# Mixing block of a hybrid decoder step: sample states on VectorE, their outputs as one wide product with ScalarE sums, convolution inputs in one tile

## The chip, the cores and the metric

The kernel runs on one core of one Trainium2 chip. The metric is device time in microseconds (us) of one execution. Five engines work side by side, each through its own queue in order: PE (TensorE, matrix products), DVE (VectorE), ACT (ScalarE), POOL (GpSimd) and SP (the queue that issues most transfers). An engine that waits holds up everything behind it in its queue.

## The reference, cut to what matters

One layer for 256 prompt tokens and 8 sample tokens (264 columns, all processed together): a SwiGLU half step, a mixing block, a second SwiGLU half step, a final norm. The mixing block runs four mLSTM heads and a short gated convolution beside each other. For a sample token, each head b updates a 256 x 256 state C and reads it with the query (one step of `mlstm_chunkwise`, length 1):

```
C_new = decay * C + wk (outer) v
num   = q . C_new
h     = num / max(|den|, exp(-m))
h     = h * rsqrt(mean(h * h) + EPS)          # per head, later gated
u     = gc * xc                               # convolution input
yc    = sum(cw[j] * u_ext[:, j:j + S] for j in range(3)) + conv_b
yb    = gb * yc, then a norm over groups of 128 channels
new_buf = u_ext[:, -2:]
```

The eight samples' states make 4 heads x 8 samples x 256 x 256 float32 values, read and written once.

## The kernel before

All weights come as float32 and are split on chip into two float16 parts: a chunk (usually 128 x 8 blocks x 128) lands in `wraw`, ACT writes the high part `whi` (L178, through `high`), DVE the rest `wlo` (L186, through `low`), and PE multiplies three times per block (`three`, L224 to L226). A product of 16 blocks is two chunks of 24 matmuls. `fetch` issues transfer, `whi` and `wlo` of a chunk up to `AHEAD` (5) chunks before PE uses it; six buffers of each exist.

Everything else is placed among these products by an agenda. `at(delta, fn)` registers work, `product` calls `tick()` at its start and `tick(0.5)` in its middle, and the work due then is written into the engines' queues at that point. So 1 stands for one product, and each engine's order follows from these numbers; when a piece really runs follows from its waits.

In `mix`, the order of products is: the gates; then h0 c0 c1 h1 c2 c3 h2 c4 c5 h3 c6 c7 (a head has six products, two each for q, k and v; a convolution block three) and o0 to o7, then the output projection. Work of a head is spread over the twelve products behind its own:

- `sample_vectors` (L787 on) makes a row `r` of q, wk, decay and 1/den per sample and sends it to memory (`dr`); `sample_rows` loads it back broadcast to all partitions (`rb`); `sample_state` loads two samples' states (`cs`). There are four groups n = 0 to 3 of two samples.
- `sample_update` (L825 on) at 3.5 + 1.5 n: per sample ACT makes two products of wk with v (into `vk` and over wk itself in `rb`) and scales the state by the decay (`cs`, L835), and POOL adds the products (L839, four per group).
- `sample_output` (L841 on) at 5 + 1.5 n: POOL issues the store of `cs`; DVE multiplies the state with q and sums along the row (`jk`, L850, four per group), then multiplies by 1/den into `ha`.
- `squares`, `norm`, `scale` at 10, 11.5 and 12 give the head's norm; the squares are on POOL.

A convolution block makes its input `u` (DVE, with POOL copies of the old rows in and the new rows out), three taps (ACT, then DVE), the product with the gate (`gated`, at 3), the square on ACT (at 3.5), a column sum on PE (`sums`, at 4.5, L353), and the rest of the norm on ACT and DVE (5, 5.5, 6).

POOL's queue also issues the transfers of `dr`, `rb`, `cs` and the states' stores, in the order in which they are written.

Of the kernel before, what the change touches and what calls it, by code (L numbers as in the profile page):

```python
# [16 lines left out]
SEQ = 256  # L17
# [97 lines left out]
def step(ctx: ExitStack, tc: tile.TileContext, a: dict, bad=None):  # L115
# [6 lines left out]
    AHEAD = 5 if half_size else 3  # L122
# [377 lines left out]
def mix(tc, a, nm, n2, h, e):  # L500
# [39 lines left out]
    rows = mp.tile([8, 2 * HD + 2], F32, tag="r", name="rows")  # L540
# [9 lines left out]
    cvp = mp.tile([128, 8, 2], F32, name="cvp")  # L550
    cvs = mp.tile([128, 8, NS, 2], F32, name="cvs")
# [56 lines left out]
    class Head:  # L608
        def __init__(self, hd):
# [26 lines left out]
            self.rb, self.c = [], []  # L636
            for n in range(4):
                at(1.5 + n if n < 3 else 6, self.sample_state, n)
                at(2.5 + n if n < 3 else 6, self.sample_rows, n)
# [37 lines left out]
        def mask_decays(self):  # L677
            for sb, x in enumerate(self.ex):
                nc.gpsimd.affine_select(
                    x, x, pattern=[[1, SEQ - 128 * sb]], compare_op=ALU.is_ge,  # L680
                    fill=0.0, base=0, channel_multiplier=-1,
                )
# [102 lines left out]
        def sample_vectors(self):  # L785
            hd, pq = self.hd, self.pq
            self.vs = vs = mp.tile([128, 2, NS], F32, tag="vs", name="vs", bufs=2)  # L787
            for i in range(2):
                nc.gpsimd.tensor_copy(vs[:, i, :], self.v[i][:, SEQ:T])
            r = mp.tile([8, 2 * HD + 2], F32, tag="r", name="r")  # L790
# [9 lines left out]
            junk = mp.tile([128, HD], F32, tag="jk", name="jk")[:8]  # L800
# [7 lines left out]
            nc.vector.reciprocal(r[:, 2 * HD + 1 : 2 * HD + 2], rdh)  # L808
            nc.vector.tensor_copy(r[:, 2 * HD : 2 * HD + 1], si[:, hd : hd + 1])
            self.dr = tc.dram_tile([8, 2 * HD + 2], F32, name=f"dr{hd}")  # L810
# [10 lines left out]
        def sample_rows(self, n):  # L821
            rb = mp.tile([128, 2, 2 * HD + 2], F32, tag="rb", name="rb", bufs=3)
            nc.gpsimd.dma_start(rb, self.dr[2 * n : 2 * n + 2].partition_broadcast(128))
            self.rb.append(rb)

        def sample_update(self, n):
            rb, c = self.rb[n], self.c[n]
            for b in range(2):
                wk = rb[:, b, HD : 2 * HD]
                vk = mp.tile([128, HD], F32, tag="vk", name="vk", bufs=2)  # L830
                for eb, out in enumerate((vk, wk)):
                    nc.scalar.activation(  # L832
                        out, wk, AF.Copy, scale=self.vs[:, eb, 2 * n + b : 2 * n + b + 1]
                    )
                nc.scalar.activation(  # L835
                    c[:, b], c[:, b], AF.Copy, scale=rb[:, b, 2 * HD : 2 * HD + 1]
                )
                for eb, add in enumerate((vk, wk)):
                    nc.gpsimd.tensor_tensor(c[:, b, eb], c[:, b, eb], add, op=ALU.add)  # L839

        def sample_output(self, n):  # L841
# [4 lines left out]
            num = mp.tile([128, 2, 2], F32, tag="num", name="num", bufs=2)  # L846
            jk = mp.tile([128, HD], F32, tag="jk", name="jk", bufs=1)
# [6 lines left out]
            for eb in range(2):  # L854
                nc.vector.tensor_tensor(
# [222 lines left out]
```

## Time and profile before

| | |
|---|---|
| time, median of 3 runs | 1887.6 us (1887.57 to 1887.67) |
| the profiled execution's own time | 1886.64 us |
| its span, first to last instruction | 1884.9 us |
| PE busy | 1836.8 us, 97% of the span |
| PE's granted clock, mean | 0.990 |
| DVE, ACT, POOL busy | 1193.9, 860.8, 228.7 us |
| mixing block, about | 716 to 1080 us of the span |

A time in a row is counted in us from the span's start. A row of the timeline has start, duration, engine, line of the kernel, operation, the tiles (output <- inputs) with shapes, and in brackets how long the engine had stood idle before it and what ended that. Matmuls overlap: a row shows 0.28 us for a matmul whose successor starts 0.11 us after it. The granted clock is a share of full speed: 1.00 is 2.4 GHz, 0.50 is 1.2 GHz.

### The profile page before, as it was taken

To read this page: it belongs to the slowest core of one execution; us is meant where nothing else is said; L and a number is where in the kernel's file an instruction comes from. 1 tells how busy PE (TensorE), PEld (TensorE's weight loads), DVE (VectorE), ACT (ScalarE), POOL (GpSimd) and SP (SyncE) were. 2 spreads that over 40 slices of the span, in tenths; PEclk is the share of its full clock that TensorE was granted. 3 is DMA by queue.
4 is the path that set the end of the run, shared out by engine and by line. 5 is a ranking of instruction groups with operands and counts; after the bars stand their busy time and mean duration, and the time that the engine had idled before them with its cause. 6 is when DMAs were issued, how large, how long until landed. Compare 5 with 4: busy or idle time off the path is not lost.

```text
span 1884.9 us, 38721 instructions
## 1 busy us (share of the span) xinstructions
PE 1836.8 (97%) x16107; PEld 1588.0 (84%) x16107; DVE 1193.9 (63%) x1982; ACT 860.8 (46%) x1141; POOL 228.7 (12%) x333
## 2 busy tenths in 40 slices
PE   8999999999999999999999899999999999999994
PEld 7888888888888888877888788888888888888884
DVE  8666655466665567787797866666654556665553
ACT  6444444344444444546555645444443444444441
POOL 5000000000000121435344122000000000000110
PEclk9999999999999999999999999999999999999997
DMA  7656566655665555877777565655666555655551
GB/s 262 215 197 200 190 194 198 204 190 192 201 193 188 194 190 174 279 241 255 246 243 271 185 211 191 201 196 189 199 192 202 194 197 193 196 194 191 194 189 57
DMA packets 114715, 381.14 MB, mean 202 GB/s; under 512 B 14797, under 2 KB 19997, under 8 KB 114529
## 3 DMA queue, kind: packets, MB, share of 16 engines
q1 hardware_dynamic: 106048, 350.79, 57.0%
q0 software_dynamic: 8192, 27.58, 4.3%
q8 instruction: 128, 2.10, 0.4%
q14 instruction: 59, 0.48, 0.1%
q10 hardware_dynamic: 288, 0.19, 0.1%
HBM read 366.73 MB, written 11.78 MB: 201 GB/s over the span
## 4 chain that ended last, share of the span: by engine, by line
PE 81%; DVE 10%; issue 3%; DMA 3%; ACT 2%; POOL 1%; SPq 0%; DVEq 0%; ACTq 0%; POOLq 0%
PE ps L226 27%; PE ps L224 27%; PE ps L225 27%; DVE wlo L186 3%; DMA rb<-dr 2%; DVE jk L850 2%; ACT whi L178 1%; ACT cs L835 0%; POOL cs L839 0%; DVE den L748 0%; DMA wraw<-in_w1gu 0%; DVE x L186 0%; ACT vk L832 0%; DVE h L480 0%; DVE qkv L514 0%
## 5 line engine op out<-in xcount | busy, mean ns | idle before, releaser
L186 DVE SCALAR_TENSOR_TENSOR wlo<-wraw,whi 128x1024 f16<-128x1024 f32 (+2 forms) x683 | 789.9, 1197 | 217.2 <-ACT whi L178 217.0
L226 PE MATMUL ps<-x,wlo 128*128 128x264 f16 x2752 | 761.6, 277 | 3.0 <-DVE wlo L186 3.0
L224 PE MATMUL ps<-x,whi 128*128 128x264 f16 x2752 | 761.5, 277 | 1.8 <-ACT whi L178 1.8
L225 PE MATMUL ps<-x,whi 128*128 128x264 f16 x2752 | 761.5, 277 | 0.0
L178 ACT ACTIVATE whi<-wraw 128x1024 f16<-128x1024 f32 (+2 forms) x683 | 665.8, 1016 | 175.1 <-PE ps L225 171.4
L226 PEld LDWEIGHTS <-wlo 128*128 128x128 f16 (+1 forms) x5296 | 518.9, 98 | 89.7 <-DVE wlo L186 10.2
L225 PEld LDWEIGHTS <-whi 128*128 128x128 f16 (+1 forms) x5296 | 518.9, 98 | 82.3 <-issue 1.9
L224 PEld LDWEIGHTS <-whi 128*128 128x128 f16 (+1 forms) x5296 | 518.9, 98 | 81.5 <-ACT whi L178 2.0
L224 PE MATMUL ps<-a,whi 128*128 128x264 f16 x1376 | 380.4, 276 | 0.0
L225 PE MATMUL ps<-a,whi 128*128 128x264 f16 x1376 | 380.4, 276 | 0.0
L226 PE MATMUL ps<-a,wlo 128*128 128x264 f16 x1376 | 380.4, 276 | 0.0
L226 PE MATMUL ps<-xm,wlo 128*128 128x264 f16 (+1 forms) x912 | 254.5, 279 | 4.4 <-DVE wlo L186 4.4
L224 PE MATMUL ps<-xm,whi 128*128 128x264 f16 (+1 forms) x912 | 254.7, 279 | 0.0
L225 PE MATMUL ps<-xm,whi 128*128 128x264 f16 (+1 forms) x912 | 254.6, 279 | 0.0
L178 ACT ACTIVATE a<-tc 128x264 f16<-128x264 f32 x86 | 36.3, 422 | 294.9 <-DVE tc L418 292.5
L378 POOL TENSOR_TENSOR acc<-h 128x264 f32<-128x264 f32 x3 | 1.9, 624 | 1192.2 <-DVE stat L294 589.1
L413 ACT ACTIVATE tb<-ta 128x264 f32<-128x264 f32 x86 | 36.3, 423 | 224.0 <-DVE ta L410 222.1
L425 DVE SCALAR_TENSOR_TENSOR h<-ps,h 128x264 f32<-128x264 f32 x64 | 27.7, 433 | 159.6 <-PE ps L226 159.6
L417 DVE TENSOR_TENSOR tc<-ps,rstd 128x264 f32<-128x264 f32 x86 | 37.2, 433 | 94.5 <-PE ps L226 94.5
L410 DVE TENSOR_TENSOR ta<-ps,rstd 128x264 f32<-128x264 f32 x86 | 37.2, 433 | 60.4 <-PE ps L226 60.2
L186 DVE SCALAR_TENSOR_TENSOR a<-tc,a 128x264 f16<-128x264 f32 x86 | 37.2, 433 | 42.1 <-ACT a L178 42.1
L378 POOL TENSOR_TENSOR sq<-h 128x264 f32<-128x264 f32 x52 | 33.8, 651 | 221.0 <-DVE h L425 83.2
(188 smaller groups left out, 970.1 us busy)
## 6 DMA issues: line engine op xcount, KB each, us to landing
wraw<-in_w2gu SPq DMA_DIRECT2D x172, 512.0 KB, 4.8
wraw<-in_w1gu SPq DMA_DIRECT2D x171, 512.0 KB, 5.0
wraw<-in_win SPq DMA_DIRECT2D x112, 512.0 KB, 5.5
wraw<-in_w1d SPq DMA_DIRECT2D x80, 448.0 KB, 4.1
wraw<-in_w2d SPq DMA_DIRECT2D x80, 448.0 KB, 4.1
wraw<-in_wout SPq DMA_DIRECT2D x32, 512.0 KB, 4.8
rb<-dr POOLq DMA_DIRECT2D x16, 514.0 KB, 7.1
wraw<-in_w1d SPq DMA_DIRECT2D x16, 512.0 KB, 4.4
```

The lines of the kernel that those rows point to most:

```text
L178: nc.scalar.activation(dst, src, AF.Copy, scale=scale)
L186: nc.vector.scalar_tensor_tensor(dst, src, scale, hi, op0=ALU.mult, op1=ALU.subtract)
L224: nc.tensor.matmul(ps, wh, xk[:, 0, :], start=first, stop=False)
L225: nc.tensor.matmul(ps, wh, xk[:, 1, :], start=False, stop=False)
L226: nc.tensor.matmul(ps, wl, xk[:, 0, :], start=False, stop=last)
L378: nc.gpsimd.tensor_tensor(sq, h[kb], h[kb], op=ALU.mult)
L410: nc.vector.tensor_tensor(zg, pg, norm.r, op=ALU.mult)
L413: nc.scalar.activation(sg, zg, AF.Silu)
L417: nc.vector.tensor_tensor(zu, pu, norm.r, op=ALU.mult)
L425: nc.vector.scalar_tensor_tensor(h[db], ps, 0.5 / (sw * sa[layer]), h[db], op0=ALU.mult, op1=ALU.add)
L850: nc.vector.scalar_tensor_tensor(jk, c[:, b, eb, :], 1.0, rb[:, b, :HD], op0=ALU.mult, op1=ALU.mult, accum_out=num[:, eb, b : b + 1],)
```

## The change

- `sample_update` is cut in two. `sample_decay` (ACT, at 3.5 + 1.5 n) scales the state; `sample_update` (DVE, at 4 + 1.5 n) does `cs = wk * v + cs` in one instruction per sample and half, with v as a per-partition scalar. `vk`, `vs` and the adds on POOL are gone.
- `sample_output` is cut in two. `sample_terms` (at 5 + 1.5 n) issues the store of the state and multiplies both samples' states with q in one DVE instruction over 1024 columns; `sample_output` (at 5.5 + 1.5 n) sums each 256 columns on ACT, straight into `ha`. The factor 1/den is now multiplied into q in `r`, one DVE instruction of 8 x 256 per head.
- The head's squares go from POOL to ACT (one instruction of 528 columns, at 10.5), their sum to DVE (at 11); norm and scale move from 11.5 and 12 to 12 and 13. Group 3's loads move from 6 to 6.5.
- The convolution inputs of all blocks lie in one tile `ua`; the old rows are copied in once by POOL near the start, the new rows are copied out once by ACT after the last convolution. The column sums and what follows move by half a product (4.5 to 5, 5 to 5.5, 5.5 to 6, 6 to 6.5).
- `mask_decays` masks the first 128 columns alone. `AHEAD` changes from 3 to 2 only in the second program behind the `If`, which this run does not enter.

```diff
@@ Head @@
-                at(3.5 + 1.5 * n, self.sample_update, n)
-                at(5 + 1.5 * n, self.sample_output, n)
-            at(10, self.squares)
-            at(11.5, self.norm)
-            at(12, self.scale)
+                at(3.5 + 1.5 * n, self.sample_decay, n)
+                at(4 + 1.5 * n, self.sample_update, n)
+                at(5 + 1.5 * n, self.sample_terms, n)
+                at(5.5 + 1.5 * n, self.sample_output, n)
+            at(10.5, self.squares)
+            at(11, self.add_squares)
+            at(12, self.norm)
+            at(13, self.scale)
...
-            self.vs = vs = mp.tile([128, 2, NS], F32, tag="vs", name="vs", bufs=2)
-            for i in range(2):
-                nc.gpsimd.tensor_copy(vs[:, i, :], self.v[i][:, SEQ:T])
...
-            nc.vector.reciprocal(r[:, 2 * HD + 1 : 2 * HD + 2], rdh)
+            nc.vector.reciprocal(rdh, rdh)
+            nc.vector.tensor_scalar(r[:, :HD], r[:, :HD], rdh, None, op0=ALU.mult)
...
+        def sample_decay(self, n):
+            rb, c = self.rb[n], self.c[n]
+            for b in range(2):
+                nc.scalar.activation(
+                    c[:, b], c[:, b], AF.Copy, scale=rb[:, b, 2 * HD : 2 * HD + 1]
+                )
 
         def sample_update(self, n):
             rb, c = self.rb[n], self.c[n]
             for b in range(2):
-                wk = rb[:, b, HD : 2 * HD]
-                vk = mp.tile([128, HD], F32, tag="vk", name="vk", bufs=2)
-                for eb, out in enumerate((vk, wk)):
-                    nc.scalar.activation(
-                        out, wk, AF.Copy, scale=self.vs[:, eb, 2 * n + b : 2 * n + b + 1]
+                col = SEQ + 2 * n + b
+                for eb in range(2):
+                    nc.vector.scalar_tensor_tensor(
+                        c[:, b, eb], rb[:, b, HD : 2 * HD], self.v[eb][:, col : col + 1],
+                        c[:, b, eb], op0=ALU.mult, op1=ALU.add,
                     )
-                nc.scalar.activation(
-                    c[:, b], c[:, b], AF.Copy, scale=rb[:, b, 2 * HD : 2 * HD + 1]
-                )
-                for eb, add in enumerate((vk, wk)):
-                    nc.gpsimd.tensor_tensor(c[:, b, eb], c[:, b, eb], add, op=ALU.add)
-
-        def sample_output(self, n):
+
+        def sample_terms(self, n):
...
+            self.jk[n] = jk = mp.tile([128, 2, 2, HD], F32, tag="jk", name="jk", bufs=2)
+            nc.vector.tensor_tensor(
+                jk, c, rb[:, :, :HD].unsqueeze(2).to_broadcast([128, 2, 2, HD]), op=ALU.mult
+            )
+
+        def sample_output(self, n):
             for b in range(2):
+                col = SEQ + 2 * n + b
                 for eb in range(2):
-                    nc.vector.scalar_tensor_tensor(
-                        jk, c[:, b, eb, :], 1.0, rb[:, b, :HD], op0=ALU.mult, op1=ALU.mult,
-                        accum_out=num[:, eb, b : b + 1],
+                    nc.scalar.activation(
+                        self.jk[n][:, b, eb], self.jk[n][:, b, eb], AF.Copy,
+                        accum_out=ha[self.hd][:, eb, col : col + 1],
                     )
...
         def squares(self):
-            x = ha[self.hd]
-            self.sq, sq1 = t264("rs"), t264("rs_q", 1)
-            for i, t in enumerate((self.sq, sq1)):
-                nc.gpsimd.tensor_tensor(t, x[:, i, :], x[:, i, :], op=ALU.mult)
-            nc.gpsimd.tensor_tensor(self.sq, self.sq, sq1, op=ALU.add)
+            self.sq2 = mp.tile([128, 2, T], F32, tag="sq2", name="sq2")
+            nc.scalar.activation(self.sq2, ha[self.hd], AF.Square)
@@ Conv @@
-            at(4.5, self.sums)
-            at(5, self.scale)
-            at(5.5, self.high)
-            at(6, self.low)
+            at(5, self.sums)
+            at(5.5, self.scale)
+            at(6, self.high)
+            at(6.5, self.low)
...
-            nc.gpsimd.tensor_copy(us[:, :, 0:2], buf[:, cb])
-            nc.gpsimd.tensor_copy(cvp[:, cb, :], u[:, SEQ : SEQ + 2])
-            nc.gpsimd.tensor_copy(cvs[:, cb], us[:, :, 1:3])
```

What this does to the queues is shown at head 0. First POOL, from the first load of `rb` (the rows of r, broadcast) to the second, before:

```order
L823 DMA rb<-dr_9480 128x1028
L816 DMA cs<-in_c 128x2x512
L899 MEMSET u 128x2
L901 COPY u<-buf 128x8x2
L903 COPY cvp<-u 128x2
L904 COPY cvs<-u 128x16
L718 MEMSET vt 128x2
L839 TENSOR_TENSOR cs<-cs,vk 128x256
L839 TENSOR_TENSOR cs<-cs,rb 128x256
L839 TENSOR_TENSOR cs<-cs,vk 128x256
L839 TENSOR_TENSOR cs<-cs,rb 128x256
L823 DMA rb<-dr_9480 128x1028
```

and now, on to the last load of this head:

```order
L827 DMA rb<-dr_9479 128x1026
L820 DMA cs<-in_c 128x2x512
L724 MEMSET vt 128x2
L827 DMA rb<-dr_9479 128x1026
L820 DMA cs<-in_c 128x2x512
L827 DMA rb<-dr_9479 128x1026
L849 DMA out_c_s<-cs 128x2x512 x2
L820 DMA cs<-in_c 128x2x512
L827 DMA rb<-dr_9479 128x1026
```

The second and third loads no longer stand behind additions; the fourth pair of loads stands behind the stores of groups 0 and 1.

ACT, from the copy of v that precedes the first sample group (`whi` is the high part of a weight chunk, `den` the prompt's denominator), before:

```order
L726 COPY vt<-ps 128x2x256
L832 ACTIVATE vk<-rb,vs 128x256
L832 ACTIVATE rb<-rb,vs 128x256
L835 ACTIVATE cs<-cs,rb 128x512
L832 ACTIVATE vk<-rb,vs 128x256
L832 ACTIVATE rb<-rb,vs 128x256
L835 ACTIVATE cs<-cs,rb 128x512
L917 ACTIVATE yc<-u,vecs 128x256
L917 ACTIVATE yc<-u,vecs 128x8
L178 ACTIVATE whi<-wraw 128x1024 x2
L744 ACTIVATE den<-ps 128x256
L832 ACTIVATE vk<-rb,vs 128x256
```

and now:

```order
L732 COPY vt<-ps 128x2x256
L833 ACTIVATE cs<-cs,rb 128x512 x2
L921 ACTIVATE yc<-ua,vecs 128x256
L921 ACTIVATE yc<-ua,vecs 128x8
L178 ACTIVATE whi<-wraw 128x1024 x2
L750 ACTIVATE den<-ps 128x256
L833 ACTIVATE cs<-cs,rb 128x512 x2
L178 ACTIVATE whi<-wraw 128x1024 x2
L861 ACTIVATE jk,ha_8885<-jk 128x256 x4
L936 ACTIVATE sq<-yc 128x264
L178 ACTIVATE whi<-wraw 128x1024 x2
```

The first wait for `rb` stands where it stood; two scalings follow it instead of six instructions, and four sums that wait for DVE's product stand between two pairs of `whi`.

PE, at the column sum of convolution block 1 (L353; `xm7`, `xm8` and `xm15` are the 8th, 9th and last input block of a product), before:

```order
L226 MATMUL ps_10147<-xm7_8146,wlo_9998 128x264
L353 MATMUL ps_10194<-sq_10118,ones_92 128x264
L224 LDWEIGHTS whi_10026
L224 MATMUL ps_10147<-xm8_8236,whi_10026 128x264
L225 LDWEIGHTS whi_10026
```

and now:

```order
L226 MATMUL ps_10106<-xm15_8866,wlo_9990 128x264
L353 MATMUL ps_10178<-sq_10077,ones_92 128x264
L224 LDWEIGHTS whi_10034
L224 MATMUL ps_10184<-xm0_7517,whi_10034 128x264
L225 LDWEIGHTS whi_10034
```

The sum moved from the middle of a product to its end, 24 matmuls later; the rest of PE's queue is as it was, apart from the same step of the head's sums.

## Rows read from the trace of the kernel before

**Rows 1.** The page: span, and busy time of each engine.

```profile
span 1884.9 us, 38721 instructions
PE 1836.8 (97%) x16107; PEld 1588.0 (84%) x16107; DVE 1193.9 (63%) x1982; ACT 860.8 (46%) x1141; POOL 228.7 (12%) x333
```

**Rows 2.** Stretches: busy (count) of PE, PEld, DVE, ACT, POOL; PE clock; DMA share, GB/s.

```profile
200.00:400.00 200.00, 200.00 (x1780) 173.74 (x1778) 109.71 (x156) 81.93 (x93) 0.00 (x0) 1.00 0.60 195
...
947.70:1022.10 74.40, 72.75 (x625) 62.96 (x623) 59.72 (x135) 41.62 (x64) 31.77 (x49) 1.00 0.75 252
```

**Rows 3.** Timeline of PE: where it stood idle in the mixing block.

```profile
802.20 0.29 PE L226 MATMUL ps<-xm,wlo 128*128 128x264 f16 x1 [2.20 <-DVE wlo L186]
...
808.27 0.71 PE L353 MATMUL ps<-sq,ones 128*128 128x264 f32 x2 [1.77 <-ACT sq L932]
...
879.70 0.29 PE L226 MATMUL ps<-xm,wlo 128*128 128x264 f16 x1 [1.19 <-DVE wlo L186]
...
885.76 1.25 PE L353 MATMUL ps<-sq,ones 128*128 128x264 f32 x2 [3.42 <-ACT sq L932]
...
963.04 0.71 PE L353 MATMUL ps<-sq,ones 128*128 128x264 f32 x2 [1.65 <-ACT sq L932]
...
1034.31 0.29 PE L226 MATMUL ps<-xm,wlo 128*128 128x264 f16 x1 [1.02 <-DVE wlo L186]
...
1041.84 1.21 PE L353 MATMUL ps<-sq,ones 128*128 128x264 f32 x2 [4.89 <-ACT sq L932]
```

**Rows 4.** PE busy, granted clock, DMA share and GB/s in the slow-clock stretches.

```profile
802.98:806.40 3.42, 3.42 (x17) 0.50 0.83 247
884.90:891.73 6.83, 5.96 (x25) 0.50 0.81 244
1041.91:1045.33 3.42, 3.42 (x14) 0.50 0.72 226
```

**Rows 5.** Timeline of ACT at the first two sample groups of head 0.

```profile
770.77 0.51 ACT L832 ACTIVATE vk<-rb,vs 128x256 f32<-128x256 f32 x1 [7.41 <-DMA rb<-dr]
...
780.09 0.51 ACT L832 ACTIVATE vk<-rb,vs 128x256 f32<-128x256 f32 x1 [3.11 <-DMA rb<-dr]
```

**Rows 6.** Timeline of POOL at the same place.

```profile
763.58 0.72 POOL L816 DMA_DIRECT2D cs<-in_c  x1
...
774.80 0.82 POOL L839 TENSOR_TENSOR cs<-cs,rb 128x256 f32<-128x256 f32 x1
775.57 0.54 POOL L823 DMA_DIRECT2D rb<-dr  x1
...
789.01 0.73 POOL L816 DMA_DIRECT2D cs<-in_c  x1 [4.30 <-issue]
```

**Rows 7.** Timeline of DVE from head 0's first sample group to PE's stop.

```profile
774.56 1.74 DVE L922 SCALAR_TENSOR_TENSOR yc<-u,vecs,yc 128x256 f32<-128x256 f32 x4 [5.88 <-ACT yc L917]
...
784.28 2.64 DVE L186 SCALAR_TENSOR_TENSOR wlo<-wraw,whi 128x1024 f16<-128x1024 f32 x2 [2.79 <-ACT whi L178]
...
792.68 0.41 DVE L850 SCALAR_TENSOR_TENSOR jk<-cs,rb 128x256 f32<-128x256 f32 x1
...
793.21 2.73 DVE L850 SCALAR_TENSOR_TENSOR jk<-cs,rb 128x256 f32<-128x256 f32 x1
...
800.92 2.89 DVE L186 SCALAR_TENSOR_TENSOR wlo<-wraw,whi 128x1024 f16<-128x1024 f32 x2
```

**Rows 8.** Groups by line and shape, 716 to 1081 us: busy us, mean ns | idle before.

```profile
L186 DVE SCALAR_TENSOR_TENSOR wlo<-wraw,whi 128x1024 f16<-128x1024 f32 x112 | 134.2, 1239 | 14.9 <-ACT whi L178 14.7
L850 DVE SCALAR_TENSOR_TENSOR jk<-cs,rb 128x256 f32<-128x256 f32 x64 | 40.7, 637 | 5.0
L835 ACT ACTIVATE cs<-cs,rb 128x512 f32<-128x512 f32 x32 | 22.6, 706 | 0.0
L832 ACT ACTIVATE vk<-rb,vs 128x256 f32<-128x256 f32 x32 | 15.9, 497 | 33.1 <-DMA rb<-dr 33.1
L726 ACT COPY vt<-ps 128x512 f32<-128x512 f32 x4 | 2.3, 587 | 0.0
L673 ACT ACTIVATE ex<-ex 128x256 f32<-128x256 f32 x4 | 1.7, 417 | 9.6 <-DVE ex L669 9.6
```

**Rows 9.** The page's transfers: queue, count, KB each, median us from issue to landing.

```profile
rb<-dr POOLq DMA_DIRECT2D x16, 514.0 KB, 7.1
```

More of the change, by code (lines that the diff above doesn't have):

```diff
@@ L121, in step @@
     sa = SA if half_size else {"1": 1.0, "2": 1.0}
-    AHEAD = 5 if half_size else 3
+    AHEAD = 5 if half_size else 2
     const = ctx.enter_context(tc.tile_pool(name="const", bufs=1))
@@ L539, in mix @@
     f = slice(32, 64)
-    rows = mp.tile([8, 2 * HD + 2], F32, tag="r", name="rows")
+    rows = mp.tile([8, 2 * HD + 1], F32, tag="r", name="rows")
     rows = rows[:4, : 2 * SEQ].rearrange("p (j t) -> p j t", j=2)
@@ L549, in mix @@
     nc.gpsimd.dma_start(buf, a["conv0"])
-    cvp = mp.tile([128, 8, 2], F32, name="cvp")
-    cvs = mp.tile([128, 8, NS, 2], F32, name="cvs")
+    ua = mp.tile([128, 8, SEQ + 2 + 3 * NS], F32, name="ua")
+    uas = ua[:, :, SEQ + 2 :].rearrange("p c (b j) -> p c b j", j=3)
+    nc.gpsimd.memset(ua[:, :, 0:2], 0.0)
+    at(2, lambda: nc.gpsimd.tensor_copy(uas[:, :, :, 0:2], buf))
     def gates_cap():
@@ L635, in __init__ @@
             at(7, self.keep_state)
[L636 removed]
+            self.rb, self.c, self.jk = [], [], {}
             for n in range(4):
[L638 to L644 removed]
+                at(1.5 + n if n < 3 else 6.5, self.sample_state, n)
+                at(2.5 + n if n < 3 else 6.5, self.sample_rows, n)
+                at(3.5 + 1.5 * n, self.sample_decay, n)
[6 more added lines that the diff above has]
+            at(13, self.scale)
         def load_decays(self):
@@ L677, in mask_decays @@
         def mask_decays(self):
-            for sb, x in enumerate(self.ex):
+            for x in self.ex:
                 nc.gpsimd.affine_select(
-                    x, x, pattern=[[1, SEQ - 128 * sb]], compare_op=ALU.is_ge,
+                    x[:, :128], x[:, :128], pattern=[[1, 128]], compare_op=ALU.is_ge,
                     fill=0.0, base=0, channel_multiplier=-1,
@@ L799, in sample_vectors @@
             )
-            junk = mp.tile([128, HD], F32, tag="jk", name="jk")[:8]
+            junk = mp.tile([8, HD], F32, tag="jk8", name="jk8")
             rdh = rd[:, hd : hd + 1]
@@ L845, in sample_output, with add_squares @@
             )
-            num = mp.tile([128, 2, 2], F32, tag="num", name="num", bufs=2)
-            jk = mp.tile([128, HD], F32, tag="jk", name="jk", bufs=1)
+            self.jk[n] = jk = mp.tile([128, 2, 2, HD], F32, tag="jk", name="jk", bufs=2)
[3 more added lines that the diff above has]
+        def sample_output(self, n):
             for b in range(2):
+                col = SEQ + 2 * n + b
                 for eb in range(2):
-                    nc.vector.scalar_tensor_tensor(
-                        jk, c[:, b, eb, :], 1.0, rb[:, b, :HD], op0=ALU.mult, op1=ALU.mult,
-                        accum_out=num[:, eb, b : b + 1],
-                    )
-            for eb in range(2):
-                nc.vector.tensor_tensor(
-                    ha[self.hd][:, eb, SEQ + 2 * n : SEQ + 2 * n + 2], num[:, eb, :],
-                    rb[:, :, 2 * HD + 1], op=ALU.mult,
-                )
-        def squares(self):
-            x = ha[self.hd]
-            self.sq, sq1 = t264("rs"), t264("rs_q", 1)
-            for i, t in enumerate((self.sq, sq1)):
-                nc.gpsimd.tensor_tensor(t, x[:, i, :], x[:, i, :], op=ALU.mult)
-            nc.gpsimd.tensor_tensor(self.sq, self.sq, sq1, op=ALU.add)
+                    nc.scalar.activation(
+                        self.jk[n][:, b, eb], self.jk[n][:, b, eb], AF.Copy,
+                        accum_out=ha[self.hd][:, eb, col : col + 1],
+                    )
+        def squares(self):
+            self.sq2 = mp.tile([128, 2, T], F32, tag="sq2", name="sq2")
+            nc.scalar.activation(self.sq2, ha[self.hd], AF.Square)
+        def add_squares(self):
+            self.sq = t264("rs")
+            nc.vector.tensor_tensor(
+                self.sq, self.sq2[:, 0, :], self.sq2[:, 1, :], op=ALU.add
+            )
         def norm(self):
@@ L964, in mix @@
         {"h": Head, "c": Conv, "o": gate}[item[0]](int(item[1]))
+    cvp = mp.tile([128, 8, 2], F32, name="cvp")
+    nc.scalar.copy(cvp, ua[:, :, SEQ : SEQ + 2])
+    cvs = mp.tile([128, 8, NS, 2], F32, name="cvs")
+    nc.scalar.copy(cvs, uas[:, :, :, 1:3])
     nc.gpsimd.dma_start(a["conv_p"], cvp)
```

10 lines of the change are left out of this document (4 added, 6 removed).

## The prediction

> **What bounds the kernel now.** The page first: PE is busy for 1836.8 of 1884.9 us [rows 1], so outside a few places PE's own work is the time. The change touches no matmul's shape or number, so it can only give back time in which PE stands still or runs slowly, and only in the mixing block. I then asked in which stretches PE is not busy; outside the block the stretches look like 200 to 400 us, where it never pauses: 1780 matmuls in 200.00 us, 0.112 us each [rows 2]. Inside the block PE's timeline shows seven stops of over one us: 2.20, 1.77, 1.19, 3.42, 1.65, 1.02 and 4.89, together 16.1 us [rows 3]. Three wait for DVE's `wlo` (weights come late), four for ACT's `sq` (the convolution's column sum L353 is asked for before it is ready). After the longer ones the granted clock reads 0.50, the lower level of 1.2 GHz, for 3.42, 6.83 and 3.42 us; PE is busy for 12.8 us of that [rows 4].
>
> What can be had: 16.1 us; seven times 0.17, because a row draws a matmul 0.28 long while its successor may start after 0.112, so 1.2; and half of 12.8, since matmuls at half clock take twice as long, 6.4. Together **23.7 us**.
>
> Why DVE and ACT are late is read at head 0. ACT stands 7.41 us before its first sample instruction and 3.11 before the second group's, both for `rb` [rows 5]; 33.1 us in all four heads [rows 8]. Behind it in ACT's queue stand the `whi` parts, so DVE stands too, 5.88 and 2.79 [rows 7]. That alone does not stop PE: it has chunks in reserve. It stops some 25 us later, because DVE cannot catch up: one `jk` takes 2.73 us where its neighbour takes 0.41, and a pair of `wlo` 2.89, at times when POOL is adding states [rows 7]; the 64 `jk` average 637 ns [rows 8].
>
> **The change part by part.**
>
> *First wait for `rb`: stays.* The scaling stands where the first product stood. `r` gets one more instruction on DVE (8 x 256; about 0.46, an estimate from the undisturbed 0.41 of a 256-column row [rows 7] plus a scalar operand), so `dr` and the first `rb` come that much later: 771.2 instead of 770.77. Behind the wait ACT has two scalings of 706 ns instead of those and four products of about 497 [rows 8]: 2.0 us less before `whi` goes on.
>
> *Second wait: mostly goes.* The second `rb` was issued at 775.57, right behind the last addition at 774.80 [rows 6], and ACT took it at 780.09. POOL now issues it behind the `cs` load of 763.58, near 764.8. It lands 7.1 us after issue by the median [rows 9], at 771.9, or, if `rb`, `cs` and `rb` follow each other at 4.5 each (775.57 to 780.09), at 780.2. ACT asks at about 775.8: 771.2, two scalings 1.4, taps 0.8, two `whi` 2.1, `den` 0.3. So the wait is between 0 and 4.4; I take 0.5, since three transfers were in that queue within 4 us at the first group as well and ACT got its `rb` 7.7 after issue.
>
> *DVE's work.* Out per group: four `jk`, 0.53 apart when undisturbed (792.68 to 793.21 [rows 7]), 2.1. In: four updates of the same shape and one product of 1024 columns. No row shows a DVE product with an operand repeated along an axis; between 1.24, the `wlo` of 1024 columns with two inputs in SBUF, and 2.55, four disturbed `jk` of 637 [rows 8]. I take 1.24, which has the same columns; updates 0.43 each, at most 0.64. A group is then 1.7 + 1.24 = 2.9 against 2.1, 0.8 more, but with POOL's additions gone nothing is left there that stretches DVE. Over a head: 59.7 busy in the period of 74.4 [rows 2], less 40.7 / 4 = 10.2, plus 16 x 0.43 + 4 x 1.24 + 0.9 (the factor in `r`, the sum of squares) = 12.8: 62.3 of a clean period of 74.4 - 1.65 - 0.17 = 72.6. About even, with 10 us to stand still in.
>
> Undisturbed rows of 256 columns from two float32 SBUF inputs take 0.41 [rows 7]. The Trainium skill, "Vector Engine (DVE) Microarchitecture Reference", section "7. Points that are easy to get wrong", says that a scalar-tensor-tensor instruction with two SBUF sources that are not bf16 runs at half throughput, which speaks against the new updates; this trace does not agree, since such an instruction is no slower there than the row above it. By the page (an estimate: 0.27 more for each of 64 updates) DVE would carry 4.3 us more per head, and the time would come out near 1869.
>
> *ACT's work.* Out per head: a quarter of 15.9, of about as much for the second product, and of 22.6, so 13.6. In: 22.6 / 4, 16 sums at 417 ns (256 columns, as `ex` [rows 8]) and 0.6 for 528 columns of squares (512 take 587 ns): 12.9. No row shows a sum on ACT; a read-out behind it may cost something, so 417 to 706 ns (twice as wide), 4.6 per head more at worst; ACT is busy 41.6 of 74.4 [rows 2], so I take 417.
>
> *The walk through head 0.* DVE's stretch from 774.56 to the end of the pair of `wlo` at 800.92 + 2.89 is 29.2 us. Less 2.79 idle, less 2.3 (the long `jk`) and 0.5 (that pair): 23.6. Less two groups of outputs, 4.2; plus three updates, 5.2, and two wide products, 2.5: 27.1. It starts at 771.2 + 0.7 = 771.9 (first scaling) and ends at 799.0 instead of 803.8: 4.8 earlier, where PE stood for 2.20. The norm's three steps, moved behind this pair, are reserve. So this stop and its two siblings go, by 2.6 us or more. With DVE's prices at their upper ends (3 x 0.85 + 2 x 1.3 = 5.2 more) the stop is back.
>
> *Column sums.* The order puts L353 24 matmuls later, 24 x 0.112 = 2.7 us. Of the four stops that alone covers 1.77 and 1.65 and leaves 0.7 and 2.2; an earlier `gated` on DVE, 5 us by the walk, covers the rest. The head's own norm (squares on ACT, 12 and 13) is needed only by the gates, whose products follow later: nothing.
>
> *Rest.* Convolution inputs, masks and copies take short work off POOL; DVE and ACT do not wait for them in any stop of rows 3: nothing. The two copies of rows at the end are 16 and 128 columns on ACT, under 0.4 each, hidden behind the last gates' chunks. I leave 1.0 for the last head, where ACT also serves the gates: between 0 and the 4.89 that stands there now, nearer 0 because both moves help.
>
> **Sum.** The span 1884.9 - 23.7 + 1.0 = 1862.2. Around the span the profiled execution has 1886.6 - 1884.9 = 1.7, and it ran 1.0 under the median of 1887.6: **1864.9 us**.
>
> **Rivals.**
>
> *One stop per head stays.* For: the second `rb` at its late bound, or ACT's sums, which wait for DVE's product while `whi` waits behind them, take back the 2.6 margin. Against: the walk has both. Price: 16.1 / 7 = 2.3, plus 0.17, plus half of the time a slow stretch of 1.7, so 3.3 x 4 = 13: 1878.
>
> *It does not do what it says.* DVE at its upper prices: the pair comes at 804 as before and only the column sums' half product is gained, some of it at once lost on the next `wlo`. 1884 to 1888, no change.
>
> *Slower: the fourth group.* Its `cs` load waits until a buffer's store has landed (4.30 us of waiting at 789.01 [rows 6]), and POOL now has the store of group 1, hence DVE's update, ahead of it. ACT's and DVE's fourth steps both stand ahead of a pair of weight parts. I place the issue near 787 and the landing at 794, when ACT asks at about 795. It decides from a landing 4 us late; at 8 late each head pays 4 idle and 3.4 of slow clock (half of 6.83), 30 in all, more than the 23.7 gained: 1894, and at 10 late 1902. Against: the store of group 0 is issued earlier than now.
>
> **How the numbers follow.** Forecast 0.60 (1861 to 1868), one stop per head 0.20 (1868 to 1882), no change 0.09, slower 0.11. About 0.2%, 3.8 us, is what a measurement can tell from no change. So faster 0.80, same 0.09, slower 0.11. The range holds the first two: 1861 (no allowance, and some of the stops below one us gone) to 1882.
>
> **What would show it.** PE's timeline from 716 to 1060 us without stops over one us and without granted clock 0.50; `wlo` near 1.22 throughout; the wide product near 1.2, updates near 0.43, sums near 0.42; the second `rb` issued within 2 us of the first and ACT's waits for it only at group 0. Wrong would be: PE waits for `wlo` or `sq` that remain; ACT waiting for DVE's product; a wide product of 2 us; ACT waiting for the fourth group's `cs`.

## The result, and the profile of the changed kernel

The changed kernel runs in 1875.1 us (median of 4, 1874.4 to 1875.9), the kernel before beside it in 1887.6: a ratio of 0.9944, interval 0.9932 to 0.9956. It is faster, by 12.5 us by the medians and 10.6 by the ratio, where the prediction had 22.7: the time lies inside the range, but the gain is about half of the forecast. The profiled execution took 1874.4 us; its page begins:

```profile
span 1872.5 us, 38560 instructions
...
PE 1830.6 (98%) x16107; PEld 1586.8 (85%) x16107; DVE 1191.9 (64%) x1910; ACT 859.6 (46%) x1211; POOL 146.8 (8%) x219
```

Against [rows 1] the span is 12.4 us shorter, while DVE and ACT are as busy as before and POOL has 82 us less. So the gain is not in less work but in where PE stands. What PE waited for between 716 and 1081 us (total, times, longest), the changed kernel:

```profile
PE ps L353 <- DVE rs L873: 8.6, 4, 6.3
PE ps L224 <- ACT xa L178: 1.3, 1, 1.3
PE ps L590 <- DVE gl L579: 0.8, 1, 0.8
```

None of the seven stops of [rows 3] is left: no wait over 0.1 us for `wlo` or `sq` (a second profile of the same kernel has one for `sq`, 0.99 us at 1027). In their place stands one that did not exist before, L353 for DVE's `rs` (L873, the sum of the head's squares), four times. PE's timeline has it once behind each head:

```profile
816.38 0.71 PE L353 MATMUL ps<-rs,ones 128*128 128x264 f32 x2 [0.48 <-DVE rs L873]
...
890.36 0.71 PE L353 MATMUL ps<-rs,ones 128*128 128x264 f32 x2 [1.26 <-DVE rs L873]
...
963.68 0.71 PE L353 MATMUL ps<-rs,ones 128*128 128x264 f32 x2 [0.60 <-DVE rs L873]
...
1043.03 1.25 PE L353 MATMUL ps<-rs,ones 128*128 128x264 f32 x2 [6.29 <-DVE rs L873]
```

Around the fourth stands the only slow stretch of the mixing block (PE, PEld, DVE, ACT and POOL busy, PE's clock, DMA share, GB/s):

```profile
1039.64:1046.47 6.83, 3.44 (x13) 2.27 (x14) 5.89 (x13) 2.87 (x5) 0.00 (x0) 0.50 0.51 171
```

By the prediction's own prices: four stops, 8.6 us, four times 0.17, and half of the 3.44 us that PE was busy at half clock make 11.0. The forecast had allowed 1.0. The span missed its forecast by 1872.5 - 1862.2 = 10.3. So this one new wait, with the clock around it, is nearly the whole miss. The question is why it came, and what would have removed it.

### The profile page after: what moved, and what is told of

The parts are those of the page before. It is cut to its first block, busy times and chain, and to the rows that moved or that the text cites. A ratio compares the mean times of both kernels' runs of the same rounds, so it can differ in the third digit from the quotient of the medians.

```text
span 1872.5 us, 38560 instructions
## 1 busy us (share of the span) xinstructions
PE 1830.6 (98%) x16107; PEld 1586.8 (85%) x16107; DVE 1191.9 (64%) x1910; ACT 859.6 (46%) x1211; POOL 146.8 (8%) x219
## 4 chain that ended last, share of the span: by engine, by line
PE 82%; DVE 9%; issue 3%; ACT 2%; DMA 2%; POOL 0%; SPq 0%; DVEq 0%; ACTq 0%; POOLq 0%
PE ps L225 27%; PE ps L224 27%; PE ps L226 27%; DVE wlo L186 3%; DMA rb<-dr 1%; DVE cs L842 1%; ACT whi L178 1%; DVE jk L853 1%; ACT jk L861 1%; ACT L329 0%; DMA wraw<-in_w1gu 0%; DVE x L186 0%; DVE qkv L514 0%; DVE h L480 0%; DVE rs_q L338 0%
## 5 line engine op out<-in xcount | busy, mean ns | idle before, releaser
L382 POOL TENSOR_TENSOR acc<-acc,sq 128x264 f32<-128x264 f32 x59 | 55.2, 936 | 6.4 <-ACT sq L376 1.8
## 6 DMA issues: line engine op xcount, KB each, us to landing
rb<-dr POOLq DMA_DIRECT2D x16, 513.0 KB, 10.2
```

Of the source, the lines that this page charges most:

```text
L382: nc.gpsimd.tensor_tensor(self.acc, self.acc, sq, op=ALU.add)
```

## The experiments

Each kernel ran in rounds beside the kernel before on its chip. The medians of before were 1884.7 to 1886.0 us there, so gains are differences of medians against the one beside it.

| kernel | us | ratio, interval | gain, us |
|---|---|---|---|
| changed kernel, again | 1875.6 | 0.9945 (0.9933 to 0.9957) | 9.5 |
| head's norm later | 1872.4 | 0.9919 (0.9906 to 0.9933) | 13.7 |
| no addition of squares on DVE | 1876.9 | 0.9952 (0.9938 to 0.9966) | 9.1 |
| that addition on POOL, norm later | 1874.3 | 0.9933 (0.9920 to 0.9947) | 11.7 |
| conv sums at the old place | 1865.9 | 0.9891 (0.9876 to 0.9906) | 20.2 |
| the same, and head's norm later | 1864.1 | 0.9895 (0.9880 to 0.9910) | 20.6 |
| conv sums old for c6, c7 alone | 1871.8 | 0.9929 (0.9916 to 0.9943) | 12.8 |
| column sum alone at the old place | 1870.3 | 0.9920 (0.9907 to 0.9933) | 15.2 |
| conv sums earlier than before | 1876.4 | 0.9952 (0.9940 to 0.9964) | 8.8 |
| before, conv sums later | 1894.7 | 1.0062 (1.0048 to 1.0076) | -10.1 |
| before, early loads of rb | 1879.0 | 0.9968 (0.9956 to 0.9980) | 5.7 |
| before, state update on DVE | 1869.1 | 0.9912 (0.9899 to 0.9926) | 16.6 |
| conv sums old, outputs on DVE | 1868.8 | 0.9907 (0.9895 to 0.9920) | 16.7 |
| conv sums old, update on POOL | 1888.3 | 1.0015 (1.0005 to 1.0024) | -2.8 |
| the same, group 3's loads earlier | 1871.8 | 0.9923 (0.9911 to 0.9936) | 13.4 |

### Is it the head's norm that stands too early?

The first theory: PE asks for the head's sum before DVE has added the squares, and that is all. Rival: ACT and DVE are late as a whole, and PE will stop at the next thing that it needs. Three kernels, each an edit of the changed one; the diffs are cut to the lines that matter. PE's request half a product later:

```diff
-            at(12, self.norm)
+            at(12.5, self.norm)
```

> The changed kernel with one number different: the head's column sum and rsqrt stand half a product later in the queues (12.5 instead of 12), 24 matmuls or 2.7 us. Theory (the missing 10 us are PE's waits for the head's sum of squares: 0.48, 1.26, 0.60 and 6.29 us, each plus 0.17, and about 1.7 from the slow clock after the last): the first three waits vanish, 2.9 us, the last shrinks to about 3.6; 5.5 to 7 us faster than the changed kernel, near 1869. Rival (the waits only show that VectorE and ScalarE are behind; PE stops on the next weights instead): PE waits for wlo or whi appear after the place and the time stays at 1874 to 1876.

No addition at all, PE sums both halves itself:

```diff
-            at(11, self.add_squares)
...
-            self.newton = rsqrt(self.rs, column_sums(self.sq), HD, later=True)
+            self.newton = rsqrt(self.rs, column_sums(self.sq2[:, 0, :], self.sq2[:, 1, :]), HD, later=True)
```

> The changed kernel without VectorE's addition of the two halves of squares: PE sums both halves into one bank, at 12 as in the changed kernel. Each head costs PE one more float32 product of 264 columns (0.66 us, as the pair of rows of one column sum shows), 2.6 in all. Theory: PE now waits for ScalarE's squares alone, which ended 4.4 us before the addition at head 3 (1038.58 against 1042.97): the three short waits vanish, the last falls from 6.29 to about 1.9, the slow clock goes: 11 - 1.9 - 2.6 = 6 to 7 us faster than the changed kernel, near 1868.5. Rival: no gain, or the 2.6 us lost.

The addition on POOL, and the request later:

```diff
-            at(12, self.norm)
+            at(12.5, self.norm)
...
-            nc.vector.tensor_tensor(
+            nc.gpsimd.tensor_tensor(
```

> The changed kernel with the sum of squares added on GpSimd instead of VectorE and the column sum at 12.5. GpSimd's queue is free there, so the sum is ready about 0.8 us after ScalarE's squares (1039.4 at head 3), and PE asks 2.7 us later than before (1039.4). Theory: all four waits and the slow clock go, 10 to 11 us faster than the changed kernel, 1864 to 1865.5, which is where the forecast of the whole change stood. Rival: PE's lateness comes out at weights, 1870 or more.

Measured: 1872.4, 1876.9 and 1874.3. The short waits of heads 0 to 2 went, but none came near 1865. The later request alone brought about 4 of the ten us. Without DVE's addition nothing was gained, though PE makes a second product for each head there, 2.6 us in all by the expectation. With the addition on POOL, PE stopped for other things instead:

```profile
PE ps L224 <- ACT xa L178: 3.9, 1, 3.9
PE ps L353 <- ACT sq L936: 3.4, 3, 1.5
PE ps L226 <- DVE wlo L186: 2.9, 3, 1.2
```

The rival holds in the main: the addition is where lateness is met first, and most of it is met again behind it. The first theory has a part of the time, but "that is all" falls.

### The half product of the convolution's sums

The part that the prediction had booked as a pure gain is undone in the changed kernel, all else kept:

```diff
-            at(5, self.sums)
-            at(5.5, self.scale)
-            at(6, self.high)
-            at(6.5, self.low)
+            at(4.5, self.sums)
+            at(5, self.scale)
+            at(5.5, self.high)
+            at(6, self.low)
```

> The changed kernel with the convolution's column sum, scale, high and low part at 4.5, 5, 5.5 and 6 as in the kernel before. By the prediction the half product covers part of four waits that were 1.77, 3.42, 1.65 and 4.89 us; the earlier gate product on VectorE (5 us by the walk) covers the rest. If the earlier VectorE alone is enough, the time stays within 1.5 us of the changed kernel; if the half product is needed, PE waits for sq come back with up to 2.7 us each at the second convolution of a head, 3 to 10 us slower than the changed kernel.

1865.9 us: ten us faster than the changed kernel, and near the forecast of 1864.9. Neither expectation had it; they had the same time or a slower one. PE's waits in the block, conv sums at the old place:

```profile
PE ps L224 <- ACT xa L178: 2.5, 1, 2.5
PE ps L353 <- DVE rs L873: 1.0, 1, 1.0
PE ps L590 <- DVE gl L579: 0.7, 1, 0.7
```

No wait for `sq` came back, so the half product had nothing left to cover. At head 0 the product with the gate (`gated`) starts at 798.84 here, at 807.33 in the kernel before, and its square is done at 801.13, 0.56 us before PE's sum. At head 3 the square is done at 1019.07 and the sum starts at 1019.12, so there is little to spare. The opposite edit, the kernel before with only this part of the change (the same diff read backwards):

> The kernel before, and nothing changed but the convolution's column sums and what follows them: half a product later (4.5 to 5, 5 to 5.5, 5.5 to 6, 6 to 6.5), as the change has it. By the prediction's step on the column sums this covers 1.77 and 1.65 us of the four stops on sq, leaves 0.7 and 2.2 of the other two, and with the slow clock behind them gone saves about 12 us: near 1875. By the theory that the half product is paid back (what stands behind the sum on ACT and DVE is pushed into the next weight parts), the stops come back on wlo or on the head's own sum: 1884 to 1890.

1894.7, ten us slower than before and worse than both expectations. PE's waits there:

```profile
PE ps L226 <- DVE wlo L186: 6.1, 4, 3.4
PE ps L353 <- POOL rs L866: 6.1, 3, 2.0
PE ps L353 <- ACT sq L932: 4.7, 3, 2.2
```

The waits for `sq` did shrink, from 11.7 [rows 3] to 4.7, as the step said. But the weights' rose from 4.4 [rows 3] to 6.1, and 6.1 for the head's sum are new. That alone only exchanges one wait for another. Two things are added: the first attention output part (`xa`), at 1087 us and so outside this view, is waited for 3.9 instead of 1.2 us, which makes the waits up to 1095 us 22.0 instead of 18.5; and there are six stretches at granted clock 0.50 of 3.41 us each, with PE busy for 20.1 us, where the kernel before has 12.8 us [rows 4]. Half of the difference is 3.7 us, so 7.2 of the 7.6 us by which the profiled execution is longer are found. Two kernels, two signs of the edit, ten us each time: the position costs, with or without the rest of the change.

**How it costs** is read behind head 0. DVE in the changed kernel, from a weight pair to the head's addition (start, duration, then as in the rows before; L335 to L341 are the Newton steps of the convolution's norm):

```profile
811.20 2.36 DVE L186 SCALAR_TENSOR_TENSOR wlo<-wraw,whi 128x1024 f16<-128x1024 f32 x2 [2.72 <-ACT whi L178]
813.48 0.62 DVE L335 SCALAR_TENSOR_TENSOR rs_q<-rs_y 128x264 f32<-128x264 f32 x1
...
815.07 0.49 DVE L945 SCALAR_TENSOR_TENSOR yc<-yc,vecs,rs 128x264 f32<-128x264 f32 x1
...
815.90 0.42 DVE L873 TENSOR_TENSOR rs<-sq 128x264 f32<-128x264 f32 x1
```

and with the sums at the old place:

```profile
807.29 0.43 DVE L335 SCALAR_TENSOR_TENSOR rs_q<-rs_y 128x264 f32<-128x264 f32 x1
...
809.74 2.36 DVE L186 SCALAR_TENSOR_TENSOR wlo<-wraw,whi 128x1024 f16<-128x1024 f32 x2 [0.55 <-ACT whi L178]
...
812.44 0.46 DVE L873 TENSOR_TENSOR rs<-sq 128x264 f32<-128x264 f32 x1
```

The steps now stand behind the pair of `wlo`, between it and the addition that PE waits for; the pair waits 2.72 us for `whi` instead of 0.55, and the addition comes 3.5 us later in the span. At the old place it ends 2.7 us before PE's sum at 815.63. Over the block DVE waits for `whi` 32.3 us instead of 20.2. ACT's waits say on which side of PE the two engines are, changed kernel first, then the old place:

```profile
ACT whi L178 <- PE ps L225: 22.7, 11, 2.9
ACT jk L861 <- DVE jk L853: 20.0, 9, 3.9
```

```profile
ACT whi L178 <- PE ps L225: 27.6, 14, 2.9
ACT rs_y L329 <- PE ps L353: 18.8, 10, 4.0
ACT jk L861 <- DVE jk L853: 15.5, 9, 3.7
```

By norm (the eight of the convolution, then the four of the heads), still at the old place:

```profile
L329 ACT ACTIVATE rs_y<-ps,eps_1.0_121 128x264 f32<-128x264 f32 x8 | 3.8, 479 | 5.8 <-PE ps L353 5.8
L329 ACT ACTIVATE rs_y<-ps,eps_1.0_119 128x264 f32<-128x264 f32 x4 | 1.9, 482 | 11.0 <-PE ps L353 11.0
```

At the old place ACT stands ready for PE's sums, 18.8 us in ten waits: 5.8 for the convolution's, 11.0 for the heads', 2.0 at a norm ahead of the block. At the new place only those 2.0 us are left: ACT is no longer ahead of PE, and what stood behind the sum falls into the next product. This shows on which side ACT is, but it does not set the price: the kernel before had only 4.0 us of this wait and lost the same ten us by the move, and the earlier position below has 21.2 and is as slow as the late one. It is worst where the gates follow. ACT in the changed kernel, at head 3:

```profile
1034.39 1.28 ACT L329 ACT_TABLE_LOAD   x1
1035.68 0.48 ACT L329 ACTIVATE rs_y<-ps,eps_1.0_121 128x264 f32<-128x264 f32 x1
1036.06 1.99 ACT L178 ACTIVATE whi<-wraw 128x1024 f16<-128x1024 f32 x2
1037.95 0.63 ACT L869 ACTIVATE sq<-ha 128x528 f32<-128x528 f32 x1
1038.60 1.28 ACT L960 ACT_TABLE_LOAD   x1
1041.68 0.42 ACT L960 ACTIVATE tb<-ta 128x264 f32<-128x264 f32 x1 [1.80 <-DVE ta L514]
```

and DVE beside it:

```profile
1037.14 2.36 DVE L186 SCALAR_TENSOR_TENSOR wlo<-wraw,whi 128x1024 f16<-128x1024 f32 x2 [3.84 <-ACT whi L178]
1039.41 0.43 DVE L335 SCALAR_TENSOR_TENSOR rs_q<-rs_y 128x264 f32<-128x264 f32 x1
...
1042.14 0.49 DVE L962 SCALAR_TENSOR_TENSOR ha<-ha,vecs,tb 128x264 f32<-128x264 f32 x1 [0.41 <-ACT tb L960]
1042.55 0.42 DVE L873 TENSOR_TENSOR rs<-sq 128x264 f32<-128x264 f32 x1
```

`rs_y` with its table load, the four sums of the last group ahead of it, the squares and the second table load fall between two sigmoids. DVE waits 3.84 us for `whi`, ACT then 1.80 for DVE's `ta`, and the addition stands behind both. The Trainium skill, "ScalarE: Activation LUTs", section "What ACT_TABLE_LOAD costs", gives 1283 ns and a drain of about 1380 for each switch. The row has the same 1.28, but `rs_y` starts 1.29 us after the load does, and the load starts 0.02 us behind the end of the last sum's read-out, so no such drain shows here.

Where in the block does it cost? The old place for the last two blocks alone:

```diff
+            d = 0 if cb >= 6 else 0.5
+            at(4.5 + d, self.sums)
```

(and the three steps behind it alike)

> The changed kernel, with the old positions of the column sums for the last two convolution blocks (c6 and c7) alone; c0 to c5 stay half a product late. If the cost of the late sums sits where the gates follow (the Newton steps of c7, the head's add queued behind them, the sigmoid's table), the 6.29 us stop at 1043 and its slow clock go and only the three short waits of heads 0 to 2 stay, 2.3 us in all: about 1868. If lateness is handed on from head to head and has to be undone in all of them: 1871 to 1875.

1871.8: about a third. The 6.29 at the gates shrank to 0.99, but the three short waits stayed and one for `sq` of 2.09 came at 1025, probably because PE asks earlier of engines that are still late from the heads before. The second expectation held: the late sums of the first six blocks cost as well. And which of its parts? Only the column sum, and ACT's `rs_y` behind it, at the old place:

```diff
-            at(5, self.sums)
+            at(4.5, self.sums)
```

> The changed kernel with the convolution's column sum alone at its old place (5 back to 4.5): PE's sum and ACT's rs_y with its table load come half a product earlier, the Newton steps, high and low parts stay late (5.5, 6, 6.5). If it is ACT's bunching (table load and rs_y beside the sample sums and the squares) that cost the late sums their time: near the version with everything back, 1866 to 1868, and the stop of 6 us at 1043 gone. If it is DVE's queue (the Newton steps ahead of the weight parts and of the head's add): 1872 to 1876, as the changed kernel.

1870.3, between both expectations: about half. The 6.29 became 3.08. So the sum with ACT's `rs_y` and DVE's steps each carry a part.

Is earlier then always better? The sums another half product ahead of the old place, beside the unchanged kernel:

```diff
-            at(4.5, self.sums)
+            at(4, self.sums)
```

(and the three steps behind it alike)

> The changed kernel with the convolution's column sums and what follows them half a product earlier than in the kernel before (4, 4.5, 5, 5.5). If only lateness costs, and ACT and DVE are ahead of PE as in the version with the old positions, where ACT waits 18.8 us for PE's sums: no stop on sq, 1864 to 1867. If the sums are then asked for before the squares are there: stops on sq of 1 to 3 us per head come back, 1868 to 1876.

> The changed kernel once more, unchanged, on the same chip as the two others: 0.9944 of the kernel before, about 1875, by which the others are read.

1876.4 and 1875.6: as bad on the other side. There PE asks before the squares are there:

```profile
PE ps L353 <- ACT sq L936: 6.6, 4, 3.0
PE ps L353 <- DVE rs L873: 2.5, 1, 2.5
```

So "late" alone is not the rule. The old place is the best of the three; half a product to either side costs ten us.

The best version with both edits, the old place and the head's norm at 12.5:

> The changed kernel with the old positions of the column sums for all blocks (1865.9 in the run before), and the head's norm half a product later (12 to 12.5). If the one wait that is left for the head's add, 0.99 us at 1034, is simply moved out of the way: 1864.9. If it only comes back at the next product that needs ACT and DVE (the first attention output part, 2.51 us, becomes longer): 1866 or more.

1864.1 (0.9895), not to be told from the old place alone (0.9891), so the time decides between neither expectation; in the trace the 0.99 went, and the wait for `xa` is 2.0 instead of 2.51, not longer. Both are faster than the kernel before by 1.1% and than the changed one by 0.5%.

### What the gain is made of

The loads of the second and third `rb` ahead of POOL's additions, in the kernel before:

```diff
-                at(2.5 + n if n < 3 else 6, self.sample_rows, n)
+                at((2.5, 3, 4, 6)[n], self.sample_rows, n)
```

> The kernel before, with POOL's load of the second and third rb issued half a product earlier, ahead of the additions of the group before; all else as before. It measures the second wait for rb by itself. By the prediction's walk the 2.79 us that DVE stands idle there are most of the 4.8 by which the weight pair comes earlier: the 2.20, 1.19 and 1.02 stops on wlo go and the stops on sq shrink by about 2.5 each, near 1874. If the stretched DVE instructions beside POOL's additions are what matters, the additions only move and the time stays within 4 us of before: 1883 to 1888.

1879.0: 5.7 us. ACT's waits for `rb` fell from 33.1 [rows 8] to 19.5 us, the first one of each head stays. The expected 1874 was too much: the `jk` beside POOL stay long (675 ns on average), and 8.6 us of waits for `sq` remain. The update alone, in the kernel before (`sample_decay` and `sample_update` of the change, outputs, squares, copies and all places as they were):

> The kernel before, with the state update of the changed kernel alone: ACT scales the states, DVE adds wk times v in one instruction per sample and half, POOL adds nothing. Outputs stay four DVE instructions, the head's squares and the copies of the convolution rows stay on POOL, the convolution sums and the head's norm stay where they were. The version with POOL's update put back into the best placement ran at 1888, so the update should carry nearly the whole gain: 1867 to 1871, as the version with DVE outputs (1868.8), if the rest (squares, copies, masks on POOL) costs nothing. If POOL's squares and copies still stretch DVE or hold up the loads of rb: 1873 to 1880. By the prediction's step on the second wait its load of rb is no longer behind additions, so that wait goes too.

1869.1: 16.6 us. If the two add up, the wait has 5.7 of it and 10.9 are the additions on POOL and ACT's products. DVE's rows there, to be read beside the 1239 and 637 of [rows 8]:

```profile
L186 DVE SCALAR_TENSOR_TENSOR wlo<-wraw,whi 128x1024 f16<-128x1024 f32 x119 | 140.0, 1216 | 7.6 <-ACT whi L178 7.5
L850 DVE SCALAR_TENSOR_TENSOR jk<-cs,rb 128x256 f32<-128x256 f32 x64 | 27.0, 423 | 1.7
```

All of the change except the wide product and the late sums (the diff is cut; four `jk` per group on DVE as before, summed straight into `ha`):

```diff
-                at(5 + 1.5 * n, self.sample_terms, n)
-                at(5.5 + 1.5 * n, self.sample_output, n)
+                at(5 + 1.5 * n, self.sample_output, n)
```

> The changed kernel with the old positions of the convolution sums (1865.9), and the sample outputs as in the kernel before: four DVE instructions per group that multiply and sum, at 5 + 1.5 n, no wide product and no sums on ACT. By the prediction's prices DVE then carries 0.9 us more per group (2.1 against 1.24), ACT 1.6 less and no wait for DVE's product. If DVE is the engine that is late: slower by about 4 to 10, 1870 to 1876. If ACT's waits for the product (20 us, 9 times, with weight parts behind them) cost as much as the wide product saves: 1864 to 1867.

1868.8, between the two expectations: as the update alone, so what else differs between the two (squares, copies, masks, the places of the head's norm and of group 3's loads) gave nothing together. Against 1865.9 the wide product brings some 3 us, if anything: the intervals overlap. The opposite test, POOL's additions put back into the version with the old place (loads of `rb` early):

> The changed kernel with the old positions of the convolution sums (1865.9), and the state update as in the kernel before: two products with v on ACT and four additions per group on POOL, behind the scaling; the loads of the second and third rb are still issued ahead of the additions, the outputs stay wide. If POOL's additions stretch DVE (the 2.73 us jk, the 2.89 us pair) and ACT's four products take room: stretched rows come back, single stops of 1 to 3 us in each head, 1873 to 1882. If the early rb was what mattered: within 3 us, 1865 to 1869.

1888.3, far more than expected. My edit had left group 3's loads behind POOL's additions of group 2, and ACT waited for them:

```profile
801.57 0.51 ACT L836 ACTIVATE vk<-rb,qkv 128x256 f32<-128x256 f32 x1 [4.14 <-DMA rb<-dr]
```

So this run mixes two causes. With those two loads at 6 instead of 6.5:

> As the version with POOL's update put back (1888.3), but the fourth group's loads of states and rb are issued ahead of the third group's additions (6 instead of 6.5), as in the kernel before; the second and third rb are early as well, so no load of rb stands behind additions. What remains against the version with the old positions of the sums (1865.9) is POOL's additions beside DVE and four products per group on ACT. If the additions stretch DVE by what the prediction says: 1873 to 1878 (the kernel before with early rb alone ran at 1879). If the fourth group's late landing was nearly all of it: 1866 to 1870.

1871.8, a little under what the stretched rows were expected to cost. Additions and products take 6.8 of the 20.2 us there, the late fourth loads another 16.2. Beside an addition, a product of DVE takes 0.95 us; all eight of this line average 0.956. DVE, then POOL, in this run, and then the same product's group in the changed kernel:

```profile
803.64 0.95 DVE L930 TENSOR_TENSOR yc<-yc,tc 128x264 f32<-128x264 f32 x1
```

```profile
803.39 0.91 POOL L843 TENSOR_TENSOR cs<-cs,vk 128x256 f32<-128x256 f32 x1
```

```profile
L932 DVE TENSOR_TENSOR yc<-yc,tc 128x264 f32<-128x264 f32 x8 | 3.4, 427 | 0.0
```

The Trainium skill, "SBUF — State Buffer", section "SBUF: two separate sides", says that a DVE instruction with two inputs in SBUF and a GpSimd one that reads SBUF lock each other out. These rows agree: 0.95 us beside an addition, 0.427 without.

## Why the prediction was half right, step by step

- **First wait for `rb`: stays.** Right at head 0. Over the four heads these first waits grew from 20.6 to 30.5 us, and all waits for `rb` from 33.1 [rows 8] to 37.5: the gain does not come from waiting less for it. Groups 0, 1 and 3 of head 0, changed kernel:

```profile
770.75 1.34 ACT L833 ACTIVATE cs<-cs,rb 128x512 f32<-128x512 f32 x2 [7.41 <-DMA rb<-dr]
...
775.66 1.33 ACT L833 ACTIVATE cs<-cs,rb 128x512 f32<-128x512 f32 x2 [0.64 <-DMA rb<-dr]
...
797.31 1.33 ACT L833 ACTIVATE cs<-cs,rb 128x512 f32<-128x512 f32 x2 [2.43 <-DMA rb<-dr]
```

- **Second wait: mostly goes.** Right: 0.64 left, 0.5 taken. Its load moved forward by itself is worth 5.7 us.
- **DVE's work** was right in its prices (wide product 1.24 taken, updates 0.43):

```profile
L186 DVE SCALAR_TENSOR_TENSOR wlo<-wraw,whi 128x1024 f16<-128x1024 f32 x118 | 139.0, 1219 | 32.6 <-ACT whi L178 32.3 <-issue 0.2
L842 DVE SCALAR_TENSOR_TENSOR cs<-rb,qkv,cs 128x256 f32<-128x256 f32 x64 | 26.3, 474 | 12.3 <-ACT cs L833 12.3
L861 ACT ACTIVATE jk<-jk 128x256 f32<-128x256 f32 x64 | 25.7, 402 | 20.0 <-DVE jk L853 20.0
L853 DVE TENSOR_TENSOR jk<-cs,rb 128x1024 f32<-128x1024 f32 x16 | 19.5, 1218 | 0.0
L861 ACT ACTIVATION_READ_ACCUMULATOR jk<-jk 128x1 f32 x64 | 11.9, 186 | 0.0
```

  The 64 updates fill 26.3 us, 0.41 each, and `wlo` is back at 1.22. The prediction judged such instructions by `jk`, which is one itself; a plain product of 264 columns takes 0.427 (above), no less. So the half throughput of the Trainium skill's "Vector Engine (DVE) Microarchitecture Reference", section "7. Points that are easy to get wrong", does not show in them.
- **ACT's work.** The sums took the 402 of the row plus a read-out; from one to the next it is 0.40 us, as taken. The 20.0 us that ACT waits for the product, named as a sign of error, are there. With the outputs on DVE that wait is gone and the time is no better; but DVE has more work in that run, so what the wait costs by itself is not shown.
- **The walk through head 0.** The weight pair was forecast to end at 799.0, with 2.6 us of margin; it started at 793.97 and took 2.36, so it ended 2.7 us before the forecast. All three stops on `wlo` went.
- **Column sums: this step failed.** It counted 2.7 us by which PE asks later and nothing for what stands behind the sum. It also did not see that the earlier `gated`, 8.5 us at head 0, was enough for all four stops: with the sums at the old place there is no wait for `sq`. And where the walk says "The norm's three steps, moved behind this pair, are reserve", they only change places: at 813.48 they stand behind a pair and ahead of the addition that PE waits for. The move covered nothing and cost ten us.
- **"The head's own norm is needed only by the gates: nothing."** This sentence hid the place of the loss. The gates need the result late, but L353 stands in PE's queue at 12, and a product behind it waits whoever needs the sum. There stand the 8.6 us, though most of their cause is the step above: with the convolution's sums at the old place 1.0 is left.
- **Last head: 1.0 left.** Mis-sized as a result: 6.29 and a slow stretch. At the old place 0.99 for the head's sum, the allowance itself, and `xa` 2.5 instead of 1.2.
- **Rest: nothing.** Right, as far as the outputs-on-DVE run beside the update alone can tell.
- **Slower: the fourth group.** It did not happen. At head 0 its `rb` was issued at 786.57, as placed, and landed at 797.3 instead of 794, so ACT waited 2.43 us for it, 5.5 us over all heads; the prediction had named a wait there as a sign of error. The run in which those loads came late lost 16.2 us, so the rival was a real one.
- **"One stop per head stays"** came nearest to the time (1878), by another wait than the one it named: that the time lies in the range is luck in so far.

## What to carry to other kernels

When a request of the bottleneck engine is moved later, price the work behind its answer on the other engines as well: here `rs_y`, Newton steps and weight parts. A wait of a helper engine for the bottleneck (ACT's 18.8 us for PE's sums) tells that the helper is ahead; how much of it a move may take is for a run to say, since half a product either way cost ten us here. And a sum that nobody needs yet still stops the engine in whose queue it stands.

Change one place at a time when several are re-timed together: the state update on DVE alone gave 16.6 us, the change without the late sums 20.2, and the late sums, four numbers, took ten of them back.

## What the runs showed of the hardware

- A product of 1024 float32 columns with one operand repeated along an axis takes 1218 ns on DVE, as one with two plain operands (1219).
- A sum on ACT leaves a second row, the accumulator's read-out of 186 ns; starts of neighbouring sums lie 0.40 us apart.
- With less in POOL's queue, `rb` landed later after its issue, 10.2 us by the median instead of 7.1 [rows 9], perhaps because three loads of states and three of `rb` are now issued within 5.5 us at each head (not tested).
